# A relu row sum on one core: the last four rows in four loads, and GpSimd at the end

## The chip, the cores and the metric

The kernel runs on one core of one Trainium2 chip. The metric is the device time of an execution in microseconds, taken as the median of several runs. A hardware profile of one further execution gives a span (first to last recorded instruction) and the times inside it.

## What is computed

The input is 32 x 512 rows of 1024 float32 values; the output is one number per row, the sum of its positive values.

```python
def reference(x):                       # x: (32, 512, 1024) float32
    relu_x = np.maximum(x, 0)
    return np.sum(relu_x, axis=-1).astype(np.float32)
```

## The kernel before

The 16,384 rows are spread over the 128 partitions, 128 rows to a partition. Row m of a partition is column m of `res`, the tile of sums (128 x 128). A "row" in this text is such a row of all partitions at once: 128 x 1024 float32, 512 KB. The 128 rows are worked in eight blocks of 16: seven in the main loop and the eighth as the tail. Three buffers of 16 rows, `io0` to `io2`, are used in turn.

**Loads and stores.** SyncE (SP) issues every transfer, in program order, on one queue. `load` (L96) issues one load with a semaphore of its own. The load of a block waits until the block three before it is summed. `store` (L105) waits on SP for a count of ScalarE (ACT) operations (L108) and then, with the DMA itself (L109), for a count of VectorE (DVE) operations; all stores count up one semaphore, `stored`.

**Main loop (L157).** For most rows ACT replaces a group of rows by its positive part (`clamp`, L116), and DVE sums the group (`total`, L124). The sixth and seventh block give some rows to ACT alone (`act_row`, L131, relu with a running sum) and the seventh the rest to DVE alone (`dve_row`, L141, the same in one instruction). An instruction that sums as it goes is followed by a short one that reads the accumulator.

**The tail (L182 to L196).** The eighth block comes in loads of 8, 4, 2 and 1 rows (`TAIL`), which ACT and DVE share row by row. The last row comes in four pieces of 244, 252, 260 and 268 columns (`PIECES`), each in a tile of its own. DVE sums the first three pieces into three extra columns behind the fourth piece (L206); the last operation (L209) then takes the fourth piece and these three sums together, 271 columns, and gives the sum of the row. It waits for its piece (L207) and for the operation before it.

**The stores.** The first block's 16 sums are stored after the tail's loads have been issued; then the sums of all rows but these and the last two (L202); and at the end those of the last two rows (L219), once ACT and DVE have finished.

**The end (L38 to L46).** The tile framework's own closing instructions are taken out and replaced. After the last store's issue SP counts up `issued` (L220). GpSimd (POOL) waits for that (L44), drains (L45) and clears all semaphores but `stored` (L46). SP waits until all stores have landed and takes `stored` back to zero (L40). The first load is moved ahead of the opening barrier (L47).

Of the kernel before, what the change touches and what calls it, by code (L numbers as in the profile page):

```python
# [4 lines left out]
F32 = mybir.dt.float32  # L5
RELU = mybir.ActivationFunctionType.Relu
MAX, ADD = mybir.AluOpType.max, mybir.AluOpType.add
P = 128

ROWS = 16  # L10
# [3 lines left out]
TWO = [[16], [16], [16], [8, 8], [8, 8], [7, 7], []]  # L14
ACT = [0, 0, 0, 0, 0, 2, 9]
DVE = [0, 0, 0, 0, 0, 0, 7]

TAIL = [8, 4, 2, 1]
PIECES = [244, 252, 260, 268]

EARLY = 1

# [1 line left out]
def kernel(tc: tile.TileContext, x: bass.AP, out: bass.AP):  # L24
    nc = tc.nc
    sems = Semaphores(tc)

    tc.close()
    tc.compile()
    nc.cur_bb = nc.bb_map[tc.start_bb_name]  # L30
    body = nc.cur_bb.bb.instructions
    ends = list(body)
    body.clear()
    n_stores = relu_sum(nc, sems, x, out)
    body.extend(ends)


    nc.cur_bb = nc.bb_map[tc.start_bb_name + "_end"]  # L38
    nc.cur_bb.bb.instructions.clear()
    nc.sync.wait_ge(sems.stored, 16 * n_stores).then_inc(sems.stored, -16 * n_stores)  # L40
    nums = sorted(s.num for s in (*sems.loads, sems.act, sems.dve, sems.issued))
    cleared = range(nums[0], nums[-1] + 1)
    assert len(cleared) == len(nums)
    nc.gpsimd.wait_ge(sems.issued, 1)  # L44
    nc.gpsimd.drain(semaphore_range=cleared)  # L45
    nc.gpsimd.sem_clear(cleared)  # L46
    issue_ahead_of_the_barrier(tc, EARLY)  # L47


class Semaphores:  # L50
    def __init__(self, tc: tile.TileContext):
        n = len(TWO) + len(TAIL) + len(PIECES)
        self.loads = [tc.alloc_semaphore(f"load{i}") for i in range(n)]
        self.act = tc.alloc_semaphore("act")
        self.dve = tc.alloc_semaphore("dve")
        self.issued = tc.alloc_semaphore("issued")
        self.stored = tc.alloc_semaphore("stored")


def relu_sum(nc, sems: Semaphores, x: bass.AP, out: bass.AP):  # L60
    x_flat = x.flatten_outer_dims()
    N, D = x_flat.shape
    NT = N // P
    NB = len(TWO)
    assert N == P * NT == P * ROWS * (NB + 1)
    assert sum(TAIL) == ROWS - 1 and sum(PIECES) == D

    bufs = [nc.alloc_sbuf_tensor(f"io{i}", [P, ROWS, D], F32) for i in range(NBUF)]
    res = nc.alloc_sbuf_tensor("res", [P, NT], F32)
    extra = len(PIECES) - 1  # L70
    parts = [
        nc.alloc_sbuf_tensor(f"piece{i}", [P, w + extra * (i == extra)], F32)
        for i, w in enumerate(PIECES)
    ]


# [7 lines left out]
    def rows(m, n):  # L84
        if m < ROWS:
            return xf[:, m : m + n, :]
        return xv[:, m - ROWS : m - ROWS + n, :]

    def sums(m, n):
        if m < ROWS:  # L90
            return of[:, m : m + n], res[:, m : m + n]
        return ov[:, m - ROWS : m - ROWS + n], res[:, m : m + n]
# [3 lines left out]
    def load(dst, src, after=None):  # L96
        nonlocal n_load
        dma = nc.sync.dma_start(out=dst, in_=src)  # L98
        if after:
            dma.wait_op(sems.dve, after[1], "sem-ge")  # L100
        dma.then_inc(sems.loads[n_load], 16)
        n_load += 1
        return sems.loads[n_load - 1]

    def store(m, n, act, dve):  # L105
        nonlocal n_store
        dst, src = sums(m, n)
        nc.sync.wait_ge(sems.act, act)  # L108
        nc.sync.dma_start(out=dst, in_=src).wait_op(sems.dve, dve, "sem-ge").then_inc(  # L109
            sems.stored, 16  # L110
        )
        n_store += 1
# [26 lines left out]
    def dve_row(ap, accum_out, loaded):  # L139
        nonlocal n_dve  # L140
        i = nc.vector.tensor_scalar(  # L141
            out=ap,
            in0=ap,
            scalar1=0.0,
            scalar2=None,
            op0=MAX,
            op1=ADD,
            accum_out=accum_out,
        )
        if loaded is not None:  # L150
            i.wait_op(loaded, 16, "sem-ge")
        i.then_inc(sems.dve, 1)
        n_dve += 1

    freed = []
    m = 0
    for j in range(NB):  # L157
        buf = bufs[j % NBUF]
        loaded = load(buf[:, :, :], rows(m, ROWS), j >= NBUF and freed[j - NBUF])
        c = 0  # L160
# [19 lines left out]
    buf = bufs[NB % NBUF]  # L180
    c = 0
    for n in TAIL:  # L182
        loaded = load(
            buf[:, c : c + n, :], rows(m, n), None if c else freed[NB - NBUF]
        )
        for i in range(n):
# [3 lines left out]
                dve_row(buf[:, c, :], res[:, m : m + 1], loaded if i == 1 else None)  # L190
            c += 1
            m += 1
    col = 0
    arrived = []
    for part, w in zip(parts, PIECES):
        arrived.append(load(part[:, :w], rows(m, 1)[:, 0, col : col + w]))  # L196
        col += w

    store(0, ROWS, *freed[0])
    store(ROWS, NT - ROWS - 2, n_act - 1, n_dve)  # L202

    last, w = parts[-1], PIECES[-1]
    for i in range(extra):
        dve_row(parts[i][:, :], last[:, w + i : w + i + 1], arrived[i])  # L206
    nc.vector.wait_ge(arrived[-1], 16)  # L207
    before_last = n_dve
    nc.vector.tensor_scalar(  # L209
# [3 lines left out]
        scalar2=None,  # L213
        op0=MAX,
        op1=ADD,
        accum_out=res[:, NT - 1 : NT],
    ).wait_op(sems.dve, before_last, "sem-ge").then_inc(sems.dve, 1)
    n_dve += 1
    store(NT - 2, 2, n_act, n_dve)  # L219
    nc.sync.sem_inc(sems.issued, 1)  # L220
    return n_store


def issue_ahead_of_the_barrier(tc: tile.TileContext, n_loads: int):


    SP = mybir.EngineType.SP
    blocks = tc.nc.main_func.blocks
    opening = blocks[0].instructions
    body = next(b for b in blocks if b.name == tc.start_bb_name).instructions  # L230
    loads = [i for i in body if i.engine == SP][:n_loads]
    for i in loads:
        assert isinstance(i, mybir.InstDMACopy)
        body.remove(i)
    at = next(
        n
        for n, i in enumerate(opening)
        if i.engine == SP and isinstance(i, mybir.InstDrain)
    )
    opening[at:at] = loads  # L240
# [30 lines left out]
```

## Time and profile before

| What | Value |
|---|---|
| Median of three runs | 161.37 us (161.32 to 161.45) |
| The profiled execution's own time | 161.37 us |
| Its span | 160.0 us |
| DVE busy | 117.7 us (74%) |
| ACT busy | 104.2 us (65%) |
| POOL busy | 0.2 us |
| Data moved | 67.18 MB, 420 GB/s over the span |
| Queue busy | 98.0% of 16 DMA engines' span |

The span is the time between the first and the last recorded instruction; the execution's own time is longer by 1.37 us, which no instruction of the kernel accounts for. Busy times leave out waits, semaphore instructions and the issuing of DMAs. "SPq", "POOLq" and "DVEq" name the instruction queues of these engines, where waits and DMA issues stand. In the DMA table a load's time counts from its issue to its landing, so a load queued behind others shows their time too.

### The profile page before, as it was taken

To read this page: it belongs to the slowest core of one execution; us is meant where nothing else is said; L and a number is where in the kernel's file an instruction comes from. 1 tells how busy PE (TensorE), PEld (TensorE's weight loads), DVE (VectorE), ACT (ScalarE), POOL (GpSimd) and SP (SyncE) were. 2 spreads that over 40 slices of the span, in tenths; PEclk is the share of its full clock that TensorE was granted. 3 is DMA by queue.
4 is the path that set the end of the run, shared out by engine and by line. 5 is a ranking of instruction groups with operands and counts; after the bars stand their busy time and mean duration, and the time that the engine had idled before them with its cause. 6 is when DMAs were issued, how large, how long until landed. Compare 5 with 4: busy or idle time off the path is not lost.

```text
span 160.0 us, 135 instructions
## 1 busy us (share of the span) xinstructions
DVE 117.7 (74%) x43; ACT 104.2 (65%) x50; POOL 0.2 (0%) x4
## 2 busy tenths in 40 slices
DVE  0000000009999499994999999999999999999995
ACT  3000049990699808996099951999339992499993
POOL 0000000000000000000000000000000000000000
DMA  7996996996996997999979969969969969898993
GB/s 262 524 508 279 524 492 295 524 491 295 524 491 295 524 442 344 524 393 393 524 344 442 524 262 524 524 262 524 524 262 524 491 295 524 377 410 385 428 405 109
DMA packets 2592, 67.18 MB, mean 420 GB/s; under 512 B 672, under 2 KB 1184, under 8 KB 1312
## 3 DMA queue, kind: packets, MB, share of 16 engines
q1 hardware_dynamic: 2592, 67.18, 98.0%
HBM read 67.11 MB, written 0.07 MB: 420 GB/s over the span
## 4 chain that ended last, share of the span: by engine, by line
DMA 43%; DVE 33%; ACT 17%; another core or an unknown queue 3%; SPq 1%; issue 0%
DVE res L124 32%; DMA io<-in_x_dram 25%; DMA piece<-in_x_dram 18%; ACT io L116 17%; SPq L98 1%; DVE piece L141 1%; DVE piece L209 0%
## 5 line engine op out<-in xcount | busy, mean ns | idle before, releaser
L124 DVE TENSOR_REDUCE res<-io 128x8 f32<-128x8192 f32 (+2 forms) x9 | 101.1, 11291 | 40.2 <-ACT io L116 40.2
L116 ACT ACTIVATE io<-io 128x8192 f32<-128x8192 f32 (+2 forms) x9 | 81.7, 9111 | 47.2 <-DMA io<-in_x_dram 47.2
L131 ACT ACTIVATE io<-io 128x1024 f32<-128x1024 f32 x20 | 20.9, 1045 | 5.4 <-DMA io<-in_x_dram 5.3
L141 DVE TENSOR_SCALAR_CACHE_REDUCE io<-io 128x1024 f32<-128x1024 f32 x13 | 15.1, 1225 | 0.2
L131 ACT ACTIVATION_READ_ACCUMULATOR io<-io 128x1 f32 x20 | 3.7, 187 | 0.0
L116 ACT ACT_TABLE_LOAD x1 | 1.3, 1283 | 0.8 <-PEq L255 0.8
L141 DVE TENSOR_SCALAR_CACHE_REDUCE piece<-piece 128x244 f32<-128x244 f32 (+2 forms) x3 | 1.2, 415 | 0.5 <-DMA piece<-in_x_dram 0.5
L141 DVE DVE_READ_ACCUMULATOR io<-io 128x1 f32 x13 | 1.2, 93 | 0.0
L209 DVE TENSOR_SCALAR_CACHE_REDUCE piece<-piece 128x271 f32<-128x271 f32 x1 | 0.4, 435 | 0.0
L141 DVE DVE_READ_ACCUMULATOR piece<-piece 128x1 f32 x3 | 0.2, 83 | 0.0
L255 POOL MEMSET const-bfloat16-1.0<- 128x1 bf16 x1 | 0.1, 103 | 0.0
L255 POOL MEMSET const-uint8-127<- 128x1 uint8 x1 | 0.1, 103 | 0.0
L255 POOL MEMSET const-float32-1.0<- 128x1 f32 x1 | 0.1, 100 | 0.0
L255 POOL MEMSET const-float32-0.0<- 128x1 f32 x1 | 0.1, 99 | 0.2 <-issue 0.2
L209 DVE DVE_READ_ACCUMULATOR piece<-piece 128x1 f32 x1 | 0.1, 82 | 0.0
## 6 DMA issues: line engine op xcount, KB each, us to landing
io<-in_x_dram SPq DMA_DIRECT2D x1, 4096.0 KB, 21.6
io<-in_x_dram SPq DMA_DIRECT2D x1, 2048.0 KB, 26.1
io<-in_x_dram SPq DMA_DIRECT2D x1, 1024.0 KB, 28.1
io<-in_x_dram SPq DMA_DIRECT2D x1, 512.0 KB, 28.9
piece<-in_x_dram SPq DMA_DIRECT2D x1, 134.0 KB, 28.4
piece<-in_x_dram SPq DMA_DIRECT2D x1, 130.0 KB, 28.6
piece<-in_x_dram SPq DMA_DIRECT2D x1, 126.0 KB, 28.7
piece<-in_x_dram SPq DMA_DIRECT2D x1, 122.0 KB, 28.8
```

The costliest lines, as they stand in the source:

```text
L98: dma = nc.sync.dma_start(out=dst, in_=src)
L116: i = nc.scalar.activation(out=ap, in_=ap, func=RELU)
L124: nc.vector.tensor_reduce(out=res[:, m : m + n], in_=ap, axis=mybir.AxisListType.X, op=ADD).wait_op(sems.act, n_act, "sem-ge").then_inc(se ...
L131: i = nc.scalar.activation(out=ap, in_=ap, func=RELU, accum_out=res[:, m : m + 1])
L141: i = nc.vector.tensor_scalar(out=ap, in0=ap, scalar1=0.0, scalar2=None, op0=MAX, op1=ADD, accum_out=accum_out,)
L209: nc.vector.tensor_scalar(out=last[:, :], in0=last[:, :], scalar1=0.0, scalar2=None, op0=MAX, op1=ADD, accum_out=res[:, NT - 1 : NT],).wai ...
L255: nc = _bacc.Bacc("TRN2", target_bir_lowering=False, num_devices=1)
```

## The change

Three things change.

- The tail's last four rows. `TAIL` keeps 8 and 4. One load then brings two rows and the first 360 columns of a third into the buffer, a second the fourth row, a third 260 columns of the third row and a fourth its last 404 columns. ACT takes the first and the fourth row, DVE the second and, in three parts, the third. The last DVE operation has 404 columns and two sums, 406 in all.
- The stores. The middle store waits for ACT and DVE up to the second of these four rows; the last store covers the third and the fourth row as before.
- The end. SP no longer waits for the stores. POOL waits for `stored` and then executes the framework's own two closing instructions, a drain and a clear of all the kernel's semaphores. The semaphore `issued` is gone.

```diff
-TAIL = [8, 4, 2, 1]
-PIECES = [244, 252, 260, 268]
+TAIL = [8, 4]
+PIECES = [360, 260, 404]
...
-    nc.cur_bb.bb.instructions.clear()
-    nc.sync.wait_ge(sems.stored, 16 * n_stores).then_inc(sems.stored, -16 * n_stores)
-    nums = sorted(s.num for s in (*sems.loads, sems.act, sems.dve, sems.issued))
-    cleared = range(nums[0], nums[-1] + 1)
-    assert len(cleared) == len(nums)
-    nc.gpsimd.wait_ge(sems.issued, 1)
-    nc.gpsimd.drain(semaphore_range=cleared)
-    nc.gpsimd.sem_clear(cleared)
+    body = nc.cur_bb.bb.instructions
+    clear = semaphore_clear(body)
+    body.clear()
+    nc.gpsimd.wait_ge(sems.stored, 16 * n_stores)
+    body.extend(clear)
     issue_ahead_of_the_barrier(tc, EARLY)
...
-    col = 0
+
+    first = PIECES[0]
+    loaded = load(
+        buf[:, :, :].rearrange("p c d -> p (c d)")[:, c * D : (c + 2) * D + first],
+        rows(m, 3).rearrange("p c d -> p (c d)")[:, : 2 * D + first],
+    )
+    act_row(buf[:, c, :], m, loaded)
+    dve_row(buf[:, c + 1, :], res[:, m + 1 : m + 2], loaded)
+    last_loaded = load(buf[:, c + 3, :], rows(m + 3, 1)[:, 0, :])
     arrived = []
-    for part, w in zip(parts, PIECES):
-        arrived.append(load(part[:, :w], rows(m, 1)[:, 0, col : col + w]))
+    col = first
+    for part, w in zip(parts, PIECES[1:]):
+        arrived.append(load(part[:, :w], rows(m + 2, 1)[:, 0, col : col + w]))
         col += w
+    sums_done = n_act, n_dve
+    act_row(buf[:, c + 3, :], m + 3, last_loaded)
...
     store(0, ROWS, *freed[0])
-    store(ROWS, NT - ROWS - 2, n_act - 1, n_dve)
+    store(ROWS, NT - ROWS - 2, *sums_done)
 
     last, w = parts[-1], PIECES[-1]
-    for i in range(extra):
-        dve_row(parts[i][:, :], last[:, w + i : w + i + 1], arrived[i])
+    dve_row(buf[:, c + 2, :first], last[:, w : w + 1], None)
+    for i in range(1, extra):
+        dve_row(parts[i - 1][:, :], last[:, w + i : w + i + 1], arrived[i - 1])
     nc.vector.wait_ge(arrived[-1], 16)
...
-        accum_out=res[:, NT - 1 : NT],
+        accum_out=res[:, NT - 2 : NT - 1],
     ).wait_op(sems.dve, before_last, "sem-ge").then_inc(sems.dve, 1)
     n_dve += 1
     store(NT - 2, 2, n_act, n_dve)
-    nc.sync.sem_inc(sems.issued, 1)
     return n_store
+
+
+def semaphore_clear(instructions):
+    pool = [i for i in instructions if i.engine == mybir.EngineType.Pool]
+    at = next(
+        n for n, i in enumerate(pool) if getattr(i, "is_reset_sema", False)
+    )
+    return pool[at : at + 2]
```

More of the change, by code (lines that the diff above doesn't have):

```diff
@@ L51, in __init__ @@
     def __init__(self, tc: tile.TileContext):
-        n = len(TWO) + len(TAIL) + len(PIECES)
+        n = len(TWO) + len(TAIL) + 1 + len(PIECES)
         self.loads = [tc.alloc_semaphore(f"load{i}") for i in range(n)]
@@ L55, in __init__ @@
         self.dve = tc.alloc_semaphore("dve")
-        self.issued = tc.alloc_semaphore("issued")
         self.stored = tc.alloc_semaphore("stored")
@@ L65, in relu_sum @@
     assert N == P * NT == P * ROWS * (NB + 1)
-    assert sum(TAIL) == ROWS - 1 and sum(PIECES) == D
+    assert sum(TAIL) == ROWS - 4 and sum(PIECES) == D
     bufs = [nc.alloc_sbuf_tensor(f"io{i}", [P, ROWS, D], F32) for i in range(NBUF)]
@@ L71, in relu_sum @@
     parts = [
-        nc.alloc_sbuf_tensor(f"piece{i}", [P, w + extra * (i == extra)], F32)
-        for i, w in enumerate(PIECES)
+        nc.alloc_sbuf_tensor(f"piece{i + 1}", [P, w + extra * (i + 1 == extra)], F32)
+        for i, w in enumerate(PIECES[1:])
     ]
```

## The prediction

> **What bounds the kernel now.** I read four views of the kernel before, in this order: the page's DMA rows, the chain that ended last, the timeline of the last microseconds, and the queue instructions of the closing lines. The page says whether an engine or the transfers set the pace:
>
> ```profile
> span 160.0 us, 135 instructions
> ...
> q1 hardware_dynamic: 2592, 67.18, 98.0%
> HBM read 67.11 MB, written 0.07 MB: 420 GB/s over the span
> ```
>
> The one queue is occupied for 98% of the span, while DVE is busy 74% and ACT 65%. So the kernel is a stream of loads, and only two things can move its time: how long the stream lasts, and what follows its last byte. The chain, in its last pieces (start, length, what), shows the hand-over:
>
> ```profile
> 128.06 28.83 DMA piece<-in_x_dram
> 156.89 0.03 issue
> 156.91 1.17 DVE piece L141 x6
> 158.09 0.02 issue
> 158.11 0.44 DVE piece L209 x2
> ```
>
> The first piece landed at 156.89 and from there DVE works without a gap to 158.55. The timeline of those microseconds has the row timings I need (start, length, operation, then the idle time and its releaser):
>
> ```profile
> 155.23 1.22 DVE L141 TENSOR_SCALAR_CACHE_REDUCE io<-io 128x1024 f32<-128x1024 f32 x1
> 156.53 1.06 ACT L131 ACTIVATE io<-io 128x1024 f32<-128x1024 f32 x1
> 156.91 0.41 DVE L141 TENSOR_SCALAR_CACHE_REDUCE piece<-piece 128x244 f32<-128x244 f32 x1 [0.45 <-DMA piece<-in_x_dram]
> 157.28 0.42 DVE L141 TENSOR_SCALAR_CACHE_REDUCE piece<-piece 128x252 f32<-128x252 f32 x1
> 157.65 0.42 DVE L141 TENSOR_SCALAR_CACHE_REDUCE piece<-piece 128x260 f32<-128x260 f32 x1
> 158.11 0.43 DVE L209 TENSOR_SCALAR_CACHE_REDUCE piece<-piece 128x271 f32<-128x271 f32 x1
> 158.47 0.08 DVE L209 DVE_READ_ACCUMULATOR piece<-piece 128x1 f32 x1
> 158.58 0.33 SPq L109 DMA_DIRECT2D out_dram<-res x1
> ```
>
> The last store goes out at 158.58; the issue table gives its landing:
>
> ```profile
> out_dram<-res SPq DMA_DIRECT2D x1, 55.0 KB, 1.8
> out_dram<-res SPq DMA_DIRECT2D x1, 1.0 KB, 1.4
> ```
>
> 158.58 + 1.4 = 160.0, the end of the span. The closing instructions, one by one (duration in ns, then the start in us):
>
> ```profile
> L40 SPq EVENT_SEMAPHORE  x1: 17/17/17, 160.0 to 160.0; - x1
> L45 POOLq DRAIN  x1: 88/88/88, 159.0 to 159.0; - x1
> L46 POOLq EVENT_SEMAPHORE_RANGE_CLEAR  x1: 136/136/136, 159.1 to 159.1; - x1
> ```
>
> GpSimd (POOL) clears its semaphores at 159.0 to 159.2, under the last store's flight; SyncE (SP) alone is last, with 17 ns.
>
> **What the Trainium skill says.** DMA: Bandwidth & Descriptors, section Queues, rings and completion order: each DMA engine takes descriptors in ring order, and a semaphore increment lands after that engine's earlier writes. The trace agrees: the tail's loads land in their order of issue, and the 8 KB store issued behind them at 130.11 needed 27.8 us. Perfetto Trace Analysis, section Sequencer-only Instruction (DRAIN, etc): the profile records only execution, not the wait or the semaphore's travel. So 88 and 136 ns are least values; the trace has no separate row for the rest. Runtime: NRT & Kernel Launch, section The ~15µs preamble/postamble breakdown: after the kernel a barrier waits until all engines are done. No row shows it, but the profiled execution took 161.37 us against a span of 160.0, so 1.37 us lie around the span. That time is also the median of the three runs, so I add differences of the span to 161.37.
>
> **The load stream.** A load's length is fitted from landings, read at the instruction that waited for it. Four rows (2 MB) were ready at 152.73 (a DVE row starts at 152.75). The eight rows before them landed at 147.83, issue 126.25 plus 21.6. Two rows landed at 155.21 (DVE and ACT both start at 155.23), one row at 156.51, the first piece at 156.89, the last piece at 129.55 + 28.4 = about 157.97. With r per row and a per load: four rows took 4r + a = 4.90, and the last four rows, in six loads, 4r + 6a = 157.97 - 152.73 = 5.24. Hence a = 0.07 and r = 1.21. The steps 2.48 and 1.30 (two rows, one row) give a = 0.12 instead, so a is 0.06 to 0.12. Four loads for six save 2a = **0.14 us** (0.12 to 0.24; 0 if the gap before the pieces is not per load).
>
> New landings, from 152.73: two rows and 360 columns (2.35 rows) at 152.73 + 2.84 + 0.07 = 155.64; the fourth row at 156.91; 260 columns (0.254 row) at 157.29; 404 columns (0.395 row) at **157.84**, against 157.97.
>
> **DVE's part.** It has one row, then 360, 260 and 406 columns, for one row and 244, 252, 260, 271. Start to start, a row takes 1.14 to 1.15 and a 250-column piece 0.37, so 360 columns take 0.37 + 110 x 1.0 ns = 0.48. DVE is free at 155.12, so it starts the row at 155.66, the 360 columns at 156.80 and the 260 at 157.28; these land at 157.29, so 157.31. In the kernel before the final operation began 0.46 after the start of the 260-column one, held by its wait for that sum. Here that allows 157.77; the data allow 157.84 plus about 0.05 for the wait in front of it (L207): **157.89** against 158.11. The operation itself is longer: from 244 and 1024 columns (407 and 1225 ns) a column costs 1.05 ns, so 406 columns take 435 + 135 x 1.05 = 577 ns, **+0.14**. The result is ready 0.22 - 0.14 = **0.08 us earlier**, the store issued at 158.50. If the stream saves 0.24, DVE's 157.77 caps the gain at 0.20; if it saves nothing, the longer operation leaves +0.05.
>
> **ACT's part** is two rows either way. It takes the first at 155.66 and the fourth row at 156.93; that ends at 158.18, 0.3 before DVE's result. With that cover gone it would set the store.
>
> **SP's part.** Two load issues fewer (0.45 to 0.47 each) come before a queue 28 us deep: nothing. If loads were waiting for issue, that would be 0.9. The 55 KB store now waits for the row ready at about 156.98 instead of 156.49. It is issued 0.5 later and at 1.8 lands near 158.8. Behind it SP's only work is the last store, ready at 158.50; SP is free at 157.35. The last store's packets moved at 159.25 to 159.75 in the windows, so there is no overlap: nothing; if there were, at most the 0.4 by which 1.8 exceeds 1.4.
>
> **The end.** The wait for the stores leaves SP. Two instructions of SP go (L40's 17 ns, L220's 17 ns), and POOL waits for the same count, then drains and clears. Queued behind POOL's wait are just those two; nobody in the kernel waits for them. They were covered by the store's flight and now come after it: 0.09 + 0.14, with start-to-start gaps, **+0.25 us** (0.22 from the rows alone, 0.35 if POOL sees the semaphore 0.1 later than SP). The range has 16 semaphores instead of 18, which I take at no change.
>
> **Sum.** -0.08 + 0.25 = +0.17 us: span 160.17, time **161.54**.
>
> What no row shows is what each engine does after its last instruction. POOL ended at 159.24 before, 0.78 before SP, so a POOL exit up to 0.78 longer than SP's was hidden there. Conversely SP now ends about 1.1 earlier, so a longer SP exit would be covered. I take them as equal and keep a few tenths on each side in the range.
>
> **The rivals.**
> 1. *POOL's exit is the longer one, slower.* The place is after the clear, outside the span; the price is the difference of the exits, 0 to 0.78, on top of +0.17. It is slower by over 0.2% (0.32 us) from a difference of 0.15 on. Half of the bound gives 161.37 + 0.17 + 0.39 = 161.93. For it: POOL never was last, so its exit is untested. Against it: the whole 1.37 holds start and end together. The price of 0.35 for the clear with a saving of nothing (+0.40, 161.77) ends in the same place. Chance 0.31.
> 2. *SP's exit is the longer one, faster.* If SP needs e more than POOL after its last instruction, SP was what the end waited for, and the change is +0.17 - e until SP's earlier end (1.1) is used up. At e = 0.25 the clear is hidden (161.29); from e = 0.49 on, or 0.37 with the stream's full gain of 0.20, it is faster by over 0.32 us; e = 0.6 gives 160.94. For it: SP issues all the transfers. Against it: 0.5 is a large part of the 1.37 that start and end share. Chance that it passes the bound: 0.07; a smaller e ends within it.
> 3. *The tail's order changes nothing*: final operation 0.14 longer, data 0.14 earlier, clear 0.25: +0.25, 161.62. For it: a is a small difference of rounded times. It lies within the bound.
>
> **How the numbers follow.** A measurement of this kernel can tell about 0.2%, 0.32 us, from no change. My forecast with rival 3 has 0.62 and stays within it. Slower by more than that is rival 1, 0.31; faster is rival 2, 0.07. The range runs from 161.25 (rival 2 at e = 0.29, or the stream's full gain with half the clear hidden) to 161.93 (rival 1 at half its bound).
>
> **What would show it.** The final DVE operation on 406 columns starts near 157.89 and takes 0.58; DVE idles little between 155.66 and then; the last store is issued near 158.50; the DRAIN and the range clear stand after its landing and end the span near 160.2. I am wrong if the last load lands no earlier than before, if DVE is late for the final operation, if the last store takes clearly other than 1.4 to land, or if time minus span departs from 1.37.

## The result, and the profile after

The changed kernel takes **162.0 us** (median of 6, 161.85 to 162.25) against 161.31 us (6 runs, 161.06 to 161.45) beside it: a ratio of 1.0045, 95% interval 1.0032 to 1.0058. It is slower by 0.7 us, where no clear change was forecast, and 0.07 above the top of the range. The profiled execution took 161.94 us.

The span hardly moved. The page of the changed kernel:

```profile
span 160.1 us, 129 instructions
...
q1 hardware_dynamic: 2304, 67.18, 97.8%
HBM read 67.11 MB, written 0.07 MB: 420 GB/s over the span
```

So 161.94 - 160.1 = 1.84 us now lie around the span, for 1.37 before. The page rounds the span to 0.1 us; with the 160.06 and 160.01 that the traces hold it is 1.88 and 1.36. Over the six executions the difference is 1.84 to 1.92. So about 0.5 of the 0.7 us was lost where the profile has no row.

That the span of this execution rose by only 0.05 us is in part chance: the load of four rows, which both kernels have alike, landed at 152.57 here and at 152.73 before. In the other traces it landed between 152.57 and 152.71 with the old loads behind it, and between 152.59 and 153.05 with the new.

Inside the span the end of the chain is as designed (start, length, what):

```profile
128.42 29.25 DMA piece<-in_x_dram
157.67 0.03 issue
157.70 0.02 DVEq L217
157.72 0.07 issue
157.79 0.58 DVE piece L219 x2
```

The last load sets the start of the last operation; before, DVE's own chain of small operations did, though only just (see "DVE's part" below). The timeline of DVE:

```profile
155.52 1.22 DVE L139 TENSOR_SCALAR_CACHE_REDUCE io<-io 128x1024 f32<-128x1024 f32 x1 [0.57 <-DMA io<-in_x_dram]
156.67 0.52 DVE L139 TENSOR_SCALAR_CACHE_REDUCE io<-io 128x360 f32<-128x360 f32 x1
157.18 0.42 DVE L139 TENSOR_SCALAR_CACHE_REDUCE piece<-piece 128x260 f32<-128x260 f32 x1
157.79 0.58 DVE L219 TENSOR_SCALAR_CACHE_REDUCE piece<-piece 128x406 f32<-128x406 f32 x1 [0.17 <-DMA piece<-in_x_dram]
```

The last store, from SyncE's timeline and from the issue table (us to landing at the end):

```profile
158.40 0.33 SPq L107 DMA_DIRECT2D out_dram<-res  x1
```

```profile
out_dram<-res SPq DMA_DIRECT2D x1, 1.0 KB, 1.4
```

And the closing instructions, which are now GpSimd's (ns, then start in us):

```profile
L31 POOLq DRAIN  x1: 83/83/83, 159.8 to 159.8; - x1
L31 POOLq EVENT_SEMAPHORE_RANGE_CLEAR  x1: 118/118/118, 159.9 to 159.9; - x1
```

They stand after the last store's landing (issue 158.40, 1.4 us to land) and end the span.

### The profile page after: what moved, and what is told of

Read it like the earlier page. It is cut to its first block, busy times and chain, and to the rows that moved or that the text cites. A ratio compares the mean times of both kernels' runs of the same rounds, so it can differ in the third digit from the quotient of the medians.

```text
span 160.1 us, 129 instructions
## 1 busy us (share of the span) xinstructions
DVE 117.5 (73%) x41; ACT 104.2 (65%) x50; POOL 0.2 (0%) x4
## 4 chain that ended last, share of the span: by engine, by line
DMA 44%; DVE 33%; ACT 17%; another core or an unknown queue 3%; SPq 1%; issue 0%; DVEq 0%
DVE res L122 32%; DMA io<-in_x_dram 25%; DMA piece<-in_x_dram 18%; ACT io L114 17%; SPq L96 1%; DVE piece L219 0%; DVEq L217 0%
## 5 line engine op out<-in xcount | busy, mean ns | idle before, releaser
L139 DVE TENSOR_SCALAR_CACHE_REDUCE io<-io 128x1024 f32<-128x1024 f32 (+1 forms) x14 | 15.5, 1173 | 0.6 <-DMA io<-in_x_dram 0.6
L219 DVE TENSOR_SCALAR_CACHE_REDUCE piece<-piece 128x406 f32<-128x406 f32 x1 | 0.6, 577 | 0.2 <-DMA piece<-in_x_dram 0.2
```

Source lines behind the costliest of these rows:

```text
L139: i = nc.vector.tensor_scalar(out=ap, in0=ap, scalar1=0.0, scalar2=None, op0=MAX, op1=ADD, accum_out=accum_out,)
L219: nc.vector.tensor_scalar(out=last[:, :], in0=last[:, :], scalar1=0.0, scalar2=None, op0=MAX, op1=ADD, accum_out=res[:, NT - 2 : NT - 1],) ...
```

## The experiments

Three explanations of the 0.47 us outside the span (0.52 without the rounding) were set against each other. An engine's "exit" means here the time between its last recorded instruction and the end of the execution. Theory 1: what GpSimd does after its last instruction takes longer than what SyncE does. Theory 2: the clear goes on after its record, on whatever engine. Theory 3: the new loads, or SyncE's early end, lengthen what lies around the span. In every table of times below, "around" is the median, over a kernel's executions, of time less span; for the kernel before it is 1.36 to 1.37 in every comparison. This time also holds what lies ahead of the first recorded instruction, which no row shows. The edits that matter below touch the end alone, so their differences are put down to the end.

**The two halves apart.** `tail_only` has the new loads and stores and the old end; `end_only` the old loads and the new end.

```diff
 # tail_only: the changed kernel, with (the semaphore `issued` and the range `cleared` come back too)
-    nc.gpsimd.wait_ge(sems.stored, 16 * n_stores)
-    body.extend(clear)
+    nc.sync.wait_ge(sems.stored, 16 * n_stores).then_inc(sems.stored, -16 * n_stores)
+    nc.gpsimd.wait_ge(sems.issued, 1)
+    nc.gpsimd.drain(semaphore_range=cleared)
+    nc.gpsimd.sem_clear(cleared)
 # end_only: the same edit the other way round, in the kernel before
```

> The new loads and stores of the last four rows, with the old end (GpSimd clears early, SyncE waits for the stores last). Changed kernel: span 160.1, time 161.94, so 1.84 us around the span, against 1.37 before. Theory 1 (GpSimd's exit after its last instruction is about 0.47 us longer than SyncE's) and theory 2 (the clear itself goes on for about 0.47 us after its record, on any engine) both say that the 0.47 goes away with the old end: 1.37 us around the span, span 159.85 to 159.95, time 161.2 to 161.3, some 0.1 under the kernel before. Theory 3 (SyncE, done early, or the new loads lengthen what lies around the span) says 1.84 stays: time near 161.75.

> The old loads of the last four rows with the new end (GpSimd waits for the stores, then drains and clears). Theories 1 and 2: 1.84 us around the span, span 160.2 to 160.3, time 162.05 to 162.15, that is 0.75 over before. Theory 3 in its form of the loads: 1.37 around the span, time 161.6.

`tail_only` took 161.22 us against 161.30 (ratio 1.0, interval 0.9992 to 1.0008), 1.39 around. `end_only` took 162.02 (1.0046, 1.0032 to 1.006), 1.90 around. The whole loss comes with the new end, so the new loads are not its cause. SyncE's early end is a part of the new end, and this pair leaves that half of theory 3 open. The 0.08 us between the medians of `tail_only` and the kernel before is not told apart from nothing.

**GpSimd or the clear.** `pool_waits_last` makes GpSimd's wait the last instruction, with the clear early; `sync_clears_last` makes the clear late, on SyncE.

```diff
 # pool_waits_last: the kernel before, with
-    nc.sync.wait_ge(sems.stored, 16 * n_stores).then_inc(sems.stored, -16 * n_stores)
     nc.gpsimd.wait_ge(sems.issued, 1)
     nc.gpsimd.drain(semaphore_range=cleared)
     nc.gpsimd.sem_clear(cleared)
+    nc.gpsimd.wait_ge(sems.stored, 16 * n_stores).then_inc(sems.stored, -16 * n_stores)
 # sync_clears_last: the kernel before, with this end alone (no `issued`; `cleared` takes in `stored`)
+    nc.sync.wait_ge(sems.stored, 16 * n_stores)
+    nc.sync.drain(semaphore_range=cleared)
+    nc.sync.sem_clear(cleared)
```

> The kernel before, with one step moved: the wait for the stores (and the setting back of its count) is GpSimd's last instruction in place of SyncE's; the drain and the clear stay early, before it. So GpSimd is last, but no clear is late. Theory 1: span 160.0, 1.84 us around it, time 161.8 to 161.9. Theory 2: 1.37 around it, time 161.3 to 161.4.

> The kernel before, but SyncE itself drains and clears all semaphores after its wait for the stores; GpSimd does nothing at the end. So the clear is late, but GpSimd is not last. Theory 1: span 160.2 to 160.3, 1.37 us around it, time 161.6. Theory 2: 1.84 around it, time 162.05.

`pool_waits_last` took 161.98 us (1.004, 1.0027 to 1.0053), 1.90 around. Its last instruction is a 17 ns wait:

```profile
L45 POOLq EVENT_SEMAPHORE_RANGE_CLEAR  x1: 136/136/136, 159.0 to 159.0; - x1
...
L46 POOLq EVENT_SEMAPHORE  x1: 17/17/17, 159.9 to 159.9; - x1
```

Moving one wait from SyncE to GpSimd leaves the span of the profiled execution at 159.9 and adds the half microsecond outside it. (That execution took 161.80 us, as expected; the five spans are 159.9 to 160.2, and the median lies above the expected 161.8 to 161.9.) `sync_clears_last` took 161.46 us (1.001, 1.0003 to 1.0016), 1.34 around. Its closing lines are

```profile
L44 SPq DRAIN  x1: 7/7/7, 160.0 to 160.0; - x1
L45 SPq EVENT_SEMAPHORE_RANGE_CLEAR  x1: 62/62/62, 160.0 to 160.0; - x1
```

A late clear adds nothing outside the span, on either engine. Theory 2 falls, and of theories 1 and 2 theory 1 stands. The expectation for SyncE's clear was about 0.25 us. Its two instructions record 69 ns where GpSimd's record 224; from the last store's issue to the end of the span it is 0.10 us more than before (1.527 and 1.425), and the median time rose by 0.16.

**Which engines.** `vector_waits_last`, `scalar_waits_last` and `tensor_waits_last` give the same last wait to DVE, ACT and TensorE (PE): in the edit of `pool_waits_last`, `nc.vector`, `nc.scalar` or `nc.tensor` in place of the added `nc.gpsimd`.

> The kernel before, with the wait for the stores as VectorE's last instruction in place of SyncE's. Time less span was 1.36 with SyncE last, and 1.90 with GpSimd last, whether GpSimd cleared at the end (1.90) or only waited (1.90). Theory 1a (GpSimd's own exit is long, the other engines' are like SyncE's): 1.3 to 1.45 here, time 161.2 to 161.4. Theory 1b (SyncE's exit is the short one; any other engine that ends last adds about 0.5): 1.8 to 1.95, time 161.8.

> The same with ScalarE's wait as the last instruction. Theory 1a: 1.3 to 1.45 around the span, time 161.2 to 161.4. Theory 1b: 1.8 to 1.95, time 161.8.

> The kernel before, with TensorE's wait for the stores as the last instruction. Around the span: 1.36 with SyncE last, 1.49 with VectorE, 1.55 with ScalarE, 1.90 with GpSimd. If an exit costs what these show for engines other than GpSimd: 1.35 to 1.6, time 161.3 to 161.55.

| Last engine | Around the span, us | Time, us | Ratio to before (95%) |
|---|---|---|---|
| SyncE (the kernel before) | 1.36 to 1.37 | 161.27 to 161.31 | |
| VectorE | 1.49 | 161.42 | 1.0009 (1.0003 to 1.0016) |
| ScalarE | 1.55 | 161.53 | 1.0014 (1.0007 to 1.0021) |
| TensorE | 1.68 | 161.64 | 1.0027 (1.0016 to 1.0039) |
| GpSimd (`pool_waits_last`) | 1.90 | 161.98 | 1.004 (1.0027 to 1.0053) |

Spans are on record to 0.1 us, so a single difference is known to 0.05 us only. The unrounded spans of the five profiled executions give 1.36, 1.49, 1.54, 1.67 and 1.92, in the same order.

Neither form of the theory held cleanly: it is not GpSimd alone, nor all but SyncE alike. What lies outside the span depends on which engine is last. SyncE's exit is the shortest and GpSimd's the longest, by 0.53 us. In the four rows below the first SyncE ends equally early, so its early end can explain at most the 0.13 us of VectorE, and not the 0.53 of GpSimd; how VectorE's 0.13 divides between the two was not tried. VectorE came out just above the 1.45, ScalarE inside 1.35 to 1.6 but above its own 1.45, and TensorE above its 1.6.

**Does an engine's exit count only if it is last?** `pool_busy_late` gives GpSimd something to do after its early clear, and leaves SyncE last.

```diff
     nc.gpsimd.sem_clear(cleared)
+    nc.gpsimd.memset(sems.scratch[:, :], 0.0)      # 128 x 384 float32, read by nobody
```

> The kernel before, with a memset of 128 x 384 float32 to a scratch tile on GpSimd after its early clear, so that GpSimd ends some tenths after 159.2 but before SyncE's 160.0. Nothing else changes; SyncE is still last. If the end is the latest of (last instruction + exit) over the engines, with GpSimd's exit about 0.54 longer than SyncE's, GpSimd's end counts once it is later than about 159.5: the time then is 161.3 plus how much later it is (a GpSimd end at 159.8 gives 161.6). If only the engine that ends last sets the exit (theory 1c), the time stays at 161.3.

It took 161.50 us (1.0017, 1.001 to 1.0024); the profiled execution 161.44. Its lines, GpSimd's from the timeline and SyncE's from the closing instructions:

```profile
159.16 0.42 POOL L47 MEMSET scratch<- 128x384 f32 x1 [158.72 <-SPq L222]
```

```profile
L40 SPq EVENT_SEMAPHORE  x1: 17/17/17, 159.8 to 159.8; - x1
```

SyncE is last in the span, yet the time rose. GpSimd ended at 159.58; with the 1.85 to 1.91 that are the medians of the five kernels with GpSimd last, that is 161.43 to 161.49. (The expectation's own rule, 161.3 plus what lies past 159.5, gives 161.38, a little low.) SyncE's way, 159.85 + 1.37, gives only 161.22. This is what an end gives that is the latest of "last instruction plus exit" over the engines, and it can't be SyncE's early end, since SyncE is last here. One memset of one length was tried; whether GpSimd's exit also depends on what it ran last is open. Applied to the kernel before: 159.24 + 1.9 = 161.14 for GpSimd against 161.37 for SyncE. The long exit was hidden there with 0.23 us to spare.

**The price of GpSimd's late clear.** `new_tail_pool_waits` is the changed kernel with the clear back in its early place and GpSimd's wait last; `after_again` is the changed kernel unedited.

> The changed kernel with one step moved back: GpSimd drains and clears early, as in the kernel before, and its last instruction is the wait for the stores with the setting back of their count. Against the changed kernel, run in the same call, it leaves out only the late drain and clear. If these cost what their records say, 0.2 to 0.25 us, it takes 161.75 to 161.8 where the changed kernel takes 162.0, with the same 1.85 to 1.9 us around the span. If a late clear costs nothing beside GpSimd's exit (162.02 and 161.98 with the old loads), both take 161.95 to 162.0.

> The changed kernel once more, as the partner of the run with the early clear: 161.95 to 162.05, 1.85 to 1.9 us around the span.

161.89 us (1.0042, 1.003 to 1.0055) against 162.09 (1.006, 1.0046 to 1.0074), both 1.89 to 1.91 around. Both lie some 0.1 us above their expected times. The difference of the medians, 0.20, is what the records of drain and clear say (83 + 118 ns). The old loads gave only 0.04 for the same step (162.02 and 161.98). With five runs each, which spread over 0.1 to 0.4 us, and intervals that overlap, the medians do not settle the size. The traces do so inside the span: from the last store's issue to the end of the span it is 1.68 us in `end_only` against 1.44 in `pool_waits_last`, and 1.65 and 1.66 in the two traces of the changed kernel against 1.43 in `new_tail_pool_waits`. That is 0.22 to 0.24 us for the late drain and clear.

**The price of a load.** `tail_six_loads` is `tail_only` with the last two loads cut in halves.

```diff
-PIECES = [360, 260, 404]
+PIECES = [360, 130, 130, 202, 202]
```

> The new loads with the old end, with 260 and 404 columns cut into 130, 130, 202 and 202: six loads for the last four rows again, with the same bytes. If a load costs 0.07 us of the stream beside its bytes, the last load is ready at about 157.84 where it was ready at 157.70 with four loads; at 0.12 per load, 157.94; if the number of loads doesn't matter, 157.70. The last operation has 206 columns (0.37 us) and may wait for VectorE, which has two more operations. Time 161.1 to 161.4.

The profiled execution had its whole tail late (four rows ready at 153.05, where `tail_only` has 152.59), so the landings are compared as intervals. From the four rows' landing to the last load's:

| Kernel | Loads | Four rows ready | Last load ready | Interval |
|---|---|---|---|---|
| before | 6 | 152.73 | 157.97 | 5.24 |
| changed | 4 | 152.57 | 157.67 | 5.10 |
| `tail_only` | 4 | 152.59 | 157.69 | 5.10 |
| `tail_six_loads` | 6 | 153.05 | 158.30 | 5.25 |

The landings are those that the traces hold for each load's semaphore. Two loads more give back the 0.14: 0.07 per load, with the same bytes. The size is less sharp than these four rows suggest. The other traces with the old six loads have 5.24 to 5.33 (and 5.51 once, in `scalar_waits_last`), the other three with four loads 5.09 to 5.11. So two loads are worth 0.13 to 0.24 us, 0.06 to 0.12 each, and the kernel before lies at the low end. Whether the load itself costs this or its shorter rows was not told apart. The time, 161.28 us (0.9999, 0.9992 to 1.0005), shows nothing of it.

**A better cut.** `tail_shifted` moves 80 columns out of the last operation, with the old end.

```diff
-PIECES = [360, 260, 404]
+PIECES = [370, 330, 324]
```

> The new loads with the old end (161.22 for 360, 260 and 404 columns), now in pieces of 370, 330 and 324 columns. There the last operation waited 0.17 us for its 404 columns and took 0.58. Here the last load lands at the same time, VectorE is ready about 0.13 later, still within that wait, and the last operation is 80 columns, 0.08 us, shorter: 161.12 to 161.18. If VectorE becomes late for it instead, 161.2 to 161.3.

It took 161.17 us (0.9994, 0.9986 to 1.0003), the lowest median of all, but not told apart from the kernel before (161.27). The timeline shows the step that was meant:

```profile
157.31 0.50 DVE L143 TENSOR_SCALAR_CACHE_REDUCE piece<-piece 128x330 f32<-128x330 f32 x1
157.85 0.49 DVE L223 TENSOR_SCALAR_CACHE_REDUCE piece<-piece 128x326 f32<-128x326 f32 x1
```

The last operation is shorter, 0.49 for 0.58, but begins 0.04 later than in `tail_only` (157.81), since DVE is now the later one. The last store goes out at 158.38, there at 158.42.

## Why the prediction was wrong

**The step that failed** is "I take them as equal": the exits of GpSimd and SyncE after their last instructions. They differ by 0.53 us. The prediction had seen that 1.37 us lie around the span and that GpSimd's exit had never been tested, and rival 1 named this mechanism, its place and its deciding point of 0.15. It had the price too low: 0.39, half of the bound of 0.78, where 0.53 was measured, and that value set the top of the range. The section of the Trainium skill that was cited (Runtime: NRT & Kernel Launch, The ~15µs preamble/postamble breakdown: the barrier waits until all engines are done) agrees with what `pool_busy_late` shows, and gives no figure per engine.

**The load stream: right.** Forecast were 0.14 us (0.12 to 0.24) saved by two loads fewer. The traces of the two kernels say 0.14, all traces but `scalar_waits_last` 0.13 to 0.24, and `tail_six_loads` gives 0.14 back.

**DVE's part: right in kind, 0.06 too good.** Forecast were a last operation of 577 ns, which is what it took, and one held by the data rather than by DVE, which it was. But from landing to start it took 0.12 us (157.67 to 157.79: the wait L217 and 0.07 of issue after it), not 0.05. The kernel before had the same wait in front of its last operation. There 157.97 + 0.12 = 158.09, and the operation began at 158.11: DVE's chain held it by 0.02 only, not by the 0.09 that the prediction's 0.05 implies. In five of the other seven traces with the old loads it began 0.12 after the landing, so there the load held it. Counted from the start of DVE's first row after the four rows' landing (152.75 before, 152.59 after), the last store goes out at 5.81 instead of 5.83: a gain of 0.02, not 0.08. The expectation of little idle time was met but for the 0.17 us ahead of the last operation.

**ACT, SP and the middle store: right.** ACT was done at 157.97, 0.4 before DVE's result. The middle store went out at 156.78 and landed after 1.6, the last found SP free, and its landing took 1.4 as before. No load waited for its issue.

**The end inside the span: about right.** Forecast 0.25 us. From the issue of the last store to the end of the span it is 1.654 us in the changed kernel (158.40 to 160.06) and 1.425 before (158.58 to 160.01), 0.23 more; the medians of `after_again` and `new_tail_pool_waits` give 0.20.

**Sum.** Of the forecast -0.08 and +0.25 inside the span, -0.02 and +0.23 were measured; to these came 0.53 outside. Together this is 0.74 against the measured 0.69, which by its interval is 0.5 to 0.9. The inside, +0.21, came near the forecast 0.17 because the two misses are small and of opposite sign (0.06 and 0.02). Rival 2 (SyncE's exit the longer) had the sign wrong; rival 3 was close to the truth for the tail.

## What to carry to other kernels

This kernel ended when the slowest of its engines was out, and the exit was not in the span. Before moving the last wait to another engine, compare execution time with span, and ask which engine was ever last; an engine that ended early shows only a bound for its exit. In this kernel the last wait belonged on SyncE, with GpSimd's clearing done under the last store's flight.

## What the runs showed of the hardware

Time less span, with each of the five engines last, was 1.36 to 1.37 (SyncE), 1.49 (VectorE), 1.55 (ScalarE), 1.68 (TensorE) and 1.90 us (GpSimd). It holds start and end together, so only the differences speak of the exits. What makes them differ was not tried. A drain and a clear of 18 semaphores recorded 7 and 62 ns on SyncE (`sync_clears_last`) and 88 and 136 ns on GpSimd (the kernel before). In the nine traces in which the last load held the last DVE operation, which stands behind a separate wait instruction, the operation started 0.12 us after the landing. Operations that carried the wait for their load themselves started 0.02 to 0.03 after it (156.89 to 156.91 in the kernel before). The last operation also carries a wait for DVE's own sums; which part of the 0.12 is whose was not tried.
